# Sixteen key and value column tiles projected ahead of the attention, two at a time, with seven block products for eight

## The chip, the cores and the metric

The kernel runs on one core of one Trainium2 chip. The metric is the device time of one execution, in microseconds (us). Five engines work side by side, each through its own queue in order: TensorE (PE, matrix products into PSUM), VectorE (DVE), ScalarE (ACT), GpSimd (POOL), and SyncE (SP), which issues nearly all transfers between HBM and SBUF. An engine whose next instruction has to wait holds back everything that stands behind it in its queue.

## The reference

One encoder layer for 512 real and 16 meta tokens (528 rows, width 2048), all in float32:

```python
hn = rmsnorm(h, pre_norm_g[layer])
proj = jnp.einsum('bld,dc->blc', hn, w_in[layer])
qa, ka, va, ga, qb, kb, vb, gb = jnp.split(proj, SPLIT_POINTS, axis=-1)
ya = gqa_axial_mixer(qa, ka, va, ...) * jax.nn.silu(ga)
yb = diff_attn_mixer(qb, kb, vb, ...) * jax.nn.silu(gb)
y = jnp.einsum('blc,cd->bld', jnp.concatenate([ya, yb], axis=-1), w_out[layer])
h = h + rmsnorm(y, post_norm_g[layer])
return h[:, N_META:, :]
```

Mixer A has 8 query heads over 2 key heads, with a norm of each head's queries and keys and a rotary embedding. Mixer B has 8 heads of differential attention: two softmaxes per head, with a bias by distance, and the second is taken away from the first with a weight. Each head is 128 wide, so keys, values, queries and gates come as column tiles of 128: `T_KA`, `T_VA`, `T_GA`, `T_QB`, `T_KB`, `T_VB` and `T_GB` are the numbers of their first tiles in `w_t`.

## The kernel before

Every float32 product is made from two parts of each operand: a rounded one (`wh`, `xh`) and the rest (`wl`, `xl`). `three` (L174) issues the three products wh·xh, wh·xl and wl·xh. `xload` (L164) loads one of 16 blocks of the transposed input, 128x528, and splits it on ACT and DVE. `wload` (L142) loads a chunk of weights 128x1024 and splits it in the same way; three such chunks are held at a time, so the split of a chunk waits for PE to be done with the third one before it.

`dense_T` (L187) projects one column tile: two chunks, 16 blocks, and for keys and values (`KEYS`, all 528 tokens) two halves of 264 columns, 96 products in all; for queries and gates (`REAL`, 512 tokens) 48 products of 512 columns. After every group of three it calls `lanes.poll()`, which puts attention work on PE between them where a task is due. The tasks are Python generators (`attention_B` L420, `attention_A` L505, `p_times_v` L375, `finish_B` L468 and the turns of keys, values and queries). Each names by a number in `LAG` how much PE time is to pass before its next piece, by the planner's own clock, which sums planned PE times. `lanes.finish` forces a task: its pieces are then put one behind the other, with no projection between them.

The kernel has these stages:

- The start (L205-L215): the first key, query and gate tiles of head B0, while the 16 input blocks come in. Then the rows of `xn` are loaded (L238-L245, tile `xns`, four buffers), squared on ACT, and made into the row scales `rt` and, by a product with ones (`spread`, L258), into `rB`, with which every projected tile is multiplied. `spread` stands on PE between the two halves of the value tile of B0.
- Mixer B (L679-L689): for each head the gate tile, then value, key and query tiles of the next head, with the attention of the current head between their products.
- The keys and values of mixer A (L691-L695); then `queries_A` (L622) for a group of four heads, 192 products of 512 columns, with its norms and rotations on ACT, DVE and POOL.
- Mixer A (L697-L709): the heads run while the second group of queries and the eight gate tiles are projected, and into the first quarter of the output projection `dense_out` (L723).
- The rest of the output projection, the last norm and the residual.

A score step of mixer A (L527-L541) is: six products into the one pair of banks `sc`, a maximum on DVE, its scaling on POOL, the exponent on ACT, a reciprocal on DVE, and the scaling of `p` on POOL. Two steps make a half: their `p` are transposed on PE, split into `ph` and `pl` (ACT and DVE), and multiplied with the values (`pv`).

## Time and profile before

| what | value |
|---|---|
| time, median of 3 runs | 958.41 us (957.73 to 959.09) |
| the profiled execution's own time | 958.46 us |
| its span | 956.5 us, 13979 instructions |
| DVE busy | 525.5 us (55%), 900 instructions |
| ACT busy | 457.9 us (48%), 812 instructions |
| POOL busy | 127.7 us (13%), 211 instructions |
| chain that ended last | PE 89%, DVE 4%, ACT 2%, DMA 2%, POOL 2% |
| largest parts of that chain | PE pd L63 55%, PE po L63 19%, PE sc L63 6%, PE pv L63 5%, PE tr L66 5% |
| HBM read and written | 91.07 MB and 7.34 MB, 103 GB/s over the span |

The span is the time from the first to the last instruction of the one execution that the hardware profiler took. L63 and L66 are helpers in which all products and transposes are issued, so tiles tell them apart: `pd` is a projection, `po` the output projection, `sc` scores, `tr` transposes, `pv` p times values. Busy times of PE overlap a little, since products are pipelined; the pace of a long run of equal products is the better measure.

### The profile page before, as it was taken

The page shows a single profiled execution, that of the slowest core. Times are in us where ns is not written, and L with a number is a line of the kernel's source. Part 1 is how long each engine was busy: PE and PEld are TensorE (multiplying, and loading weights), DVE is VectorE, ACT ScalarE, POOL GpSimd, SP SyncE. Part 2 cuts the span into 40 slices and gives each one's busy share as a digit, 9 for nine tenths or more (in the row PEclk, how much of TensorE's full clock was granted, in tenths as well). Part 3 has the DMA queues.
Part 4 walks back from the last instruction along what each step waited for, and adds up shares of the span by engine and source line. Part 5 has one row for each costly group of instructions (what it writes and reads, how often), then busy time and mean ns, then how long its engine had stood idle before and what let it go on. Part 6 is the DMA issues. An engine that isn't in the chain of part 4 may idle for free.

```text
span 956.5 us, 13979 instructions
## 1 busy us (share of the span) xinstructions
PE 934.7 (98%) x5530; PEld 818.2 (86%) x5530; DVE 525.5 (55%) x900; ACT 457.9 (48%) x812; POOL 127.7 (13%) x211
## 2 busy tenths in 40 slices
PE   7999999999999999999999999998999999999996
PEld 6889898989989898998998888886888888888884
DVE  6276675747575574756654274447554663232325
ACT  6665555547464553746552253354555742221221
POOL 0001010101001010100201041225212120000002
PEclk9999999999999999999999999998999999999999
DMA  9752222322223122222223223111222344623314
GB/s 318 252 180 77 85 90 68 97 77 94 82 73 104 66 99 77 86 82 68 91 75 94 94 66 110 57 66 56 77 77 67 114 128 158 238 88 98 101 45 175
DMA packets 31426, 99.31 MB, mean 104 GB/s; under 512 B 3681, under 2 KB 5601, under 8 KB 30721
## 3 DMA queue, kind: packets, MB, share of 16 engines
q1 hardware_dynamic: 31216, 98.42, 31.1%
q8 instruction: 43, 0.70, 0.3%
q14 instruction: 23, 0.18, 0.1%
q10 hardware_dynamic: 144, 0.01, 0.0%
HBM read 91.07 MB, written 7.34 MB: 103 GB/s over the span
## 4 chain that ended last, share of the span: by engine, by line
PE 89%; DVE 4%; ACT 2%; DMA 2%; POOL 2%; issue 1%; SPq 0%; DVEq 0%; POOLq 0%; ACTq 0%
PE pd L63 55%; PE po L63 19%; PE sc L63 6%; PE pv L63 5%; PE tr L66 5%; DMA xns<-in_xn_dram 2%; DVE qn L567 1%; DVE wl L151 1%; POOL ssh L228 1%; ACT qn L639 0%; ACT jk L564 0%; PE ss L63 0%; POOL qn L581 0%; ACT p L537 0%; DMA gcol<-in_gpre_dram 0%
## 5 line engine op out<-in xcount | busy, mean ns | idle before, releaser
L63 PE MATMUL pd<-xh,wh 128*128 128x264 f32 (+1 forms) x992 | 334.8, 337 | 4.9 <-ACT wh L150 4.9
L63 PE MATMUL pd<-xh,wl 128*128 128x264 f32 (+1 forms) x992 | 326.4, 329 | 0.3 <-DVE wl L151 0.3
L63 PE MATMUL pd<-xl,wh 128*128 128x264 f32 (+1 forms) x992 | 326.1, 329 | 0.0
L150 ACT ACTIVATE wh<-st 128x1024 fp32r<-128x1024 f32 (+2 forms) x139 | 144.4, 1039 | 278.0 <-PE po L63 95.8
L151 DVE TENSOR_TENSOR wl<-st,wh 128x1024 fp32r<-128x1024 f32 (+2 forms) x139 | 167.2, 1203 | 176.0 <-ACT wh L150 174.7
L63 PEld LDWEIGHTS pd<-xh,wh 128*128 128x128 f32 x992 | 188.4, 190 | 17.6 <-ACT wh L150 4.9
L63 PEld LDWEIGHTS pd<-xh,wl 128*128 128x128 f32 x992 | 187.7, 189 | 18.0 <-DVE wl L151 0.7
L63 PEld LDWEIGHTS pd<-xl,wh 128*128 128x128 f32 x992 | 188.6, 190 | 11.6
L63 PE MATMUL po<-wh,ol 128*128 128x512 f32 x256 | 101.0, 395 | 0.9 <-DVE ol L296 0.9
L63 PE MATMUL po<-wl,oh 128*128 128x512 f32 x256 | 101.9, 398 | 0.0
L63 PE MATMUL po<-wh,oh 128*128 128x512 f32 x256 | 101.7, 397 | 0.0
L450 ACT ACTIVATE p<-p,mx 128x528 f32<-128x528 f32 x64 | 46.5, 728 | 34.2 <-POOL mx L447 34.0
L63 PEld LDWEIGHTS po<-wh,ol 128*128 128x128 f32 x256 | 48.1, 188 | 12.2 <-DVE ol L296 1.2
L440 DVE CUSTOM_DVE_ANT_0 p<-sc,dist 128x528 f32<-128x528 f32 x64 | 44.9, 701 | 24.0 <-PE sc L63 23.5
L63 PEld LDWEIGHTS po<-wl,oh 128*128 128x128 f32 x256 | 48.1, 188 | 11.2
L63 PEld LDWEIGHTS po<-wh,oh 128*128 128x128 f32 x256 | 48.1, 188 | 10.2
L63 PE MATMUL pd<-wh,xh 128*128 128x512 f32 x128 | 52.2, 408 | 0.8 <-DVE vf L287 0.8
L293 ACT ACTIVATE ph<-tr 128x512 fp32r<-128x512 f32 x64 | 37.6, 591 | 31.2 <-PE tr L66 30.9
L296 DVE TENSOR_TENSOR pl<-tr,ph 128x512 fp32r<-128x512 f32 x64 | 43.4, 688 | 16.1 <-ACT ph L293 14.9
L66 PE MATMUL tr<-ident,p 128*128 128x128 f32 (+1 forms) x320 | 50.8, 273 | 0.8 <-DVE pl L296 0.8
L63 PE MATMUL pd<-wh,xl 128*128 128x512 f32 x128 | 50.6, 395 | 0.0
L63 PE MATMUL pd<-wl,xh 128*128 128x512 f32 x128 | 50.5, 395 | 0.0
(161 smaller groups left out, 1292.1 us busy)
## 6 DMA issues: line engine op xcount, KB each, us to landing
st<-in_w_t_dram SPq DMA_DIRECT2D x82, 512.0 KB, 3.6
st<-in_w_o_dram SPq DMA_DIRECT2D x32, 512.0 KB, 3.6
st<-in_w_q_dram SPq DMA_DIRECT2D x16, 512.0 KB, 3.6
xs<-in_xT_dram SPq DMA_DIRECT2D x16, 264.0 KB, 5.1
xns<-in_xn_dram SPq DMA_DIRECT2D x8, 512.0 KB, 6.3
xr<-in_xn_dram SPq DMA_DIRECT2D x4, 1024.0 KB, 10.2
os<-oscr SPq DMA_DIRECT2D x6, 512.0 KB, 3.6
out_dram<-y SPq DMA_DIRECT2D x6, 512.0 KB, 2.7
```

Source lines behind the costliest of these rows:

```text
L63: self._add(self.nc.tensor.matmul(out, lhsT, rhs, start=start, stop=stop), us)
L66: self._add(self.nc.tensor.transpose(out, in_, ident), 0.109)
L150: nc.scalar.activation(wh[:, c], st[:, c], AF.Copy)
L151: nc.vector.tensor_tensor(out=wl[:, c], in0=st[:, c], in1=wh[:, c].bitcast(F32), op=ALU.subtract)
L228: nc.gpsimd.tensor_tensor(out=dst, in0=dst, in1=mhalf[:rows, :dst.shape[1]], op=ALU.pow)
L293: nc.scalar.activation(dst, src, AF.Copy)
L296: nc.vector.tensor_tensor(out=dst, in0=src, in1=h.bitcast(F32), op=ALU.subtract)
L440: nc.vector.tensor_tensor_reduce(out=two(p), in0=sc[:, :, :HALF], in1=two(dist[:, w0:w0 + NT]), scale=1.0, scalar=-3.0e38, op0=ALU.add, op ...
L450: nc.scalar.activation(p2[m], p2[m], AF.Exp, scale=0.125, bias=mx[:, m:m + 1], accum_out=sm[:, m:m + 1])
L567: nc.vector.scalar_tensor_tensor(out=raw[:, i, :], in0=raw[:, i, :], scalar=ss[:rows, i:i + 1], in1=g[:rows], op0=ALU.mult, op1=ALU.mult)
```

## The change

Two column tiles a and b are taken together as a matrix of weights with 2x2 blocks, and so is the input (even and odd blocks of 128 rows, first and second 264 tokens). Their projection is formed from seven products of blocks in place of eight, in Winograd's form of Strassen's method. This is done for eight pairs of tiles: keys and values of heads B1 to B7, and the two value tiles of mixer A. It is a stage of its own (`products`), ahead of all attention: its products have no `lanes.poll()` between them.

- In the start, `xsums` forms four sums of input blocks for each pair of blocks and splits them: POOL scales the raw blocks in place, DVE takes four differences of 264 columns, ACT rounds (`th`, 128x1056), and DVE takes the rest (`tl`). The raw block `xs` is now kept until then (five buffers in place of six); `xns` shares three buffers with these sums.
- `operands` loads quarter tiles (`rw`, every second piece of 128 columns, so pieces of 512 bytes), forms the sums of weights on POOL (two of 128x1024) and DVE (two), and splits seven operands for a pair. `product` runs 24 products of 264 columns.
- The seven results are added up on ACT and DVE, scaled by `rB` on POOL (two of 128x528 for a pair), and written to HBM (`pj`). The first key, query, value and gate tiles of B0 and gate A0 are written there too. The attention loads them from there (`got`, `gate_of`).
- The tables and the attention's buffers (`ap`, `psc`, `ptr`) are opened only after this stage, on the memory that it used.
- The eight gate tiles of mixer A move: A0 to the start, A1 to A6 into the heads of mixer B (`GATES_B`, spilled to HBM and loaded again), and A7 stays. `LATE` (an empty list) and `late_gate` go.

```diff
+GATE_0 = 0
+GATES_B = {0: 1, 1: 2, 2: 3, 3: 4, 4: 5, 5: 6}
 GATES = [[0, 1], [2, 3, 4, 5, 6, 7]]
...
+    def xsums(i, r1, r2):
+        with tc.high_priority(SUMS):
+            for k, r in ((2 * i, r1), (2 * i + 1, r2)):
+                nc.gpsimd.tensor_scalar(out=r, in0=r, scalar1=gcol[:, k:k + 1], scalar2=1.0,
+                                        op0=ALU.mult, op1=ALU.mult)
+            t = sp.tile([P, 4, HALF], F32, name="ts", tag="sb", bufs=3)
+            sub = lambda o, a, b: nc.vector.tensor_tensor(out=o, in0=a, in1=b, op=ALU.subtract)
+            sub(t[:, 0, :], r1[:, HALF:], r1[:, :HALF])
+            sub(t[:, 2, :], r2[:, HALF:], r1[:, HALF:])
+            sub(t[:, 1, :], r2[:, HALF:], t[:, 0, :])
+            sub(t[:, 3, :], t[:, 1, :], r2[:, :HALF])
+            nc.scalar.activation(th[i], t, AF.Copy)
+            nc.vector.tensor_tensor(out=tl[i], in0=t, in1=th[i].bitcast(F32), op=ALU.subtract)
...
-            st = ap.tile([P, 1024], F32, name="xns", tag="ph" if j else "pl")
+            st = sp.tile([P, 4 * HALF], F32, name="xns", tag="sb", bufs=3)[:, :1024]
...
+        a11 = raw(a, 0)
+        yield split(a11)
+        a21, a22 = raw(b, 0), raw(b, 1)
+        s1 = wp.tile([P, 1024], F32, name="s1w", tag="st")
+        nc.gpsimd.tensor_tensor(out=s1, in0=a21, in1=a22, op=ALU.add)
+        yield split(s1)
+        a12 = raw(a, 1)
+        s2 = wp.tile([P, 1024], F32, name="s2w", tag="st")
+        nc.vector.tensor_tensor(out=s2, in0=s1, in1=a11, op=ALU.subtract)
+        yield split(s2)
+        yield split(a12)
+        nc.gpsimd.tensor_tensor(out=a21, in0=a11, in1=a21, op=ALU.subtract)
+        yield split(a21)
+        yield split(a22)
+        nc.vector.tensor_tensor(out=a12, in0=a12, in1=s2, op=ALU.subtract)
+        yield split(a12)
...
+        for a, b in quads:
...
+            nc.scalar.activation(u1, product(b11), AF.Copy)
+            p5 = product(lambda i: sums(i, 0))
+            tt(out=u2, in0=product(lambda i: sums(i, 1)), in1=u1, op=ALU.add)
+            tt(out=ca[:, H0], in0=product(b21), in1=u1, op=ALU.add)
+            tt(out=u3, in0=product(lambda i: sums(i, 2)), in1=u2, op=ALU.add)
+            tt(out=cb[:, H1], in0=p5, in1=u3, op=ALU.add)
+            tt(out=ca[:, H1], in0=p5, in1=u2, op=ALU.add)
+            tt(out=cb[:, H0], in0=u3, in1=product(lambda i: sums(i, 3)), op=ALU.subtract)
+            nc.gpsimd.tensor_tensor(out=cb, in0=cb, in1=rB, op=ALU.mult)
+            put(b, cb)
+            tt(out=ca[:, H1], in0=product(b22), in1=ca[:, H1], op=ALU.add)
+            nc.gpsimd.tensor_tensor(out=ca, in0=ca, in1=rB, op=ALU.mult)
+            put(a, ca)
...
+    with tc.tile_pool(name="w1", bufs=5) as w1:
+        products([(T_KB + h, T_VB + h) for h in range(1, NH)] + [(T_VA, T_VA + 1)])
+    pre.close()
...
         if h + 1 < NH:
-            pss = dense_T(KEYS)
+            pss = dense_T(REAL)
             if h:
                 finish_head(h - 1)
-            v = values(pss)
-            ks = keys_B(dense_T(KEYS))
-            qs = queries_B(dense_T(REAL))
+            v = values(got(T_VB + h + 1, "vf"))
+            ks = keys_B(got(T_KB + h + 1, "kf"))
+            qs = queries_B(scaled(pss))
+        if h in GATES_B:
+            spill_gate(GATES_B[h], gate(dense_T(REAL), "gs"))
```

Where the instructions stand, engine by engine, shows what the diff alone does not. On DVE, in the middle of the start, the queue before held only the rests of the input blocks (`xl`) and of the weight chunks (`wl`):

```order
L168 SCALAR_TENSOR_TENSOR xl_111<-xs,gcol,xh_95 128x528
L168 SCALAR_TENSOR_TENSOR xl_112<-xs,gcol,xh_96 128x528
L151 TENSOR_TENSOR wl<-st,wh 128x768
L168 SCALAR_TENSOR_TENSOR xl_113<-xs,gcol,xh_97 128x528
L168 SCALAR_TENSOR_TENSOR xl_114<-xs,gcol,xh_98 128x528
L151 TENSOR_TENSOR wl<-st,wh 128x768
```

At the same place it now also holds the differences (`ts`) and the rests of the sums (`tl`):

```order
L177 SCALAR_TENSOR_TENSOR xl_117<-xs,gcol,xh_101 128x528
L191 TENSOR_TENSOR ts<-ts,xs 128x264
L191 TENSOR_TENSOR ts<-xs 128x264 x2
L177 SCALAR_TENSOR_TENSOR xl_118<-xs,gcol,xh_102 128x528
L191 TENSOR_TENSOR ts<-xs,ts 128x264
L197 TENSOR_TENSOR tl_135<-ts,th_127 128x1056
L160 TENSOR_TENSOR wl<-st,wh 128x768
```

Between two weight chunks stand five more instructions, and they stand ahead of the chunk; counted over the whole queue, 27 differences and 6 rests of sums stand ahead of the last chunk of the start.

On SP, at the end of the start, two chunks of `w_t` and then the rows `xns` stood behind the last chunk of `w_s`:

```order
L139 DMA st<-in_w_s_dram 128x768
L139 DMA xs<-in_xT_dram 128x528
L148 DMA st<-in_w_t_dram 128x1024 x2
L139 DMA xns<-in_xn_dram 128x1024 x8
L139 DMA xns<-in_xm_dram 16x1024 x2
```

Now three chunks stand ahead of the first row tile and a fourth behind it:

```order
L148 DMA st<-in_w_s_dram 128x768
L148 DMA xs<-in_xT_dram 128x528
L157 DMA st<-in_w_t_dram 128x1024 x3
L148 DMA xns<-in_xn_dram 128x1024
L157 DMA st<-in_w_t_dram 128x1024
L148 DMA xns<-in_xn_dram 128x1024 x7
L148 DMA xns<-in_xm_dram 16x1024 x2
```

There are three buffers `st`, so the third of these chunks needs the buffer of the last chunk of `w_s`, which is free when its `wl` is made.

On PE, in mixer A behind the second group of queries, groups of three projection products (`pd`) stood between scores, transposes and `pv` all through:

```order
L63 MATMUL sc<-kl,qh 128x264
L63 MATMUL sc<-kh,qlA 128x264
L63 MATMUL pd<-wh,xh_99 128x512
L63 MATMUL pd<-wh,xl_115 128x512
L63 MATMUL pd<-wl,xh_99 128x512
L63 MATMUL pv<-ph,vh 128x256
```

In the changed kernel the same stage reads:

```order
L68 MATMUL sc<-kl,qh 128x264
L68 MATMUL sc<-kh,qlA 128x264
L71 MATMUL tr<-ident,p 128x128 x8
L71 MATMUL tr<-ident,p 32x128 x2
L68 MATMUL sc<-kh,qh 128x264
L68 MATMUL sc<-kl,qh 128x264
L68 MATMUL sc<-kh,qlA 128x264
L68 MATMUL sc<-kh,qh 128x264
L68 MATMUL sc<-kl,qh 128x264
L68 MATMUL sc<-kh,qlA 128x264
L68 MATMUL pv<-ph,vh 128x256
```

From the end of the second group's products to the gate tile A7, 13 score steps, 91 products with values (seven groups of 13) and 74 transposes stand on PE with no `pd` among them.

## The prediction

> **What bounds the kernel now.** I read the page first, then PE's chain in order of time, then busy times by stage.

> ```profile
> span 956.5 us, 13979 instructions
> PE 934.7 (98%) x5530; PEld 818.2 (86%) x5530; DVE 525.5 (55%) x900; ACT 457.9 (48%) x812; POOL 127.7 (13%) x211
> 69.64 2.92 PE pd L63 x24
> 307.20:363.10 55.90, 55.90 (x375) 51.19 (x374) 35.69 (x65) 30.24 (x49) 6.03 (x11) 1.00 0.25 85
> 579.50:660.00 80.50, 76.46 (x407) 63.72 (x406) 39.60 (x73) 36.18 (x91) 24.04 (x41) 0.96 0.21 70
> ```

> PE is busy from end to end; 24 products of 264 columns take 2.92 us, 0.1217 each. The last two rows are stretches, with the busy times of PE, its weight loads, DVE, ACT and POOL in that order, then the granted clock. A head of mixer B (55.9 us) shows no idle PE; behind the second group of queries (579.5 to 660) PE misses 4.0 us. So a product less is time less, as long as PE has other products while the other engines do the softmax. Those are what this change takes out of the attention.

> **Products.** 16 tiles x 96 = 1536 products of 264 columns become 8 pairs x 7 x 24 = 1344; all others keep number and shape. 192 x 0.1217 = **-23.4 us**.

> **The start.**

> ```profile
> 30.07 0.96 DVE L151 TENSOR_TENSOR wl<-st,wh 128x768 fp32r<-128x768 f32 x1 [1.93 <-ACT wh L150]
> 4.46:31.03 26.57, 26.14 (x131) 22.66 (x132) 18.87 (x25) 16.47 (x24) 0.00 (x0) 1.00 0.87 316
> 51.13 0.77 DVE L287 TENSOR_TENSOR kf<-pd,rB 128x264 f32<-128x264 f32 x2
> L151 DVE TENSOR_TENSOR wl<-st,wh 128x1024 fp32r<-128x1024 f32 x130 | 159.4, 1226 | 168.7 <-ACT wh L150 167.5 <-PE tr L66 0.3
> 605.89 0.71 POOL L540 TENSOR_SCALAR p<-p,smA 128x528 f32<-128x528 f32 x1 [1.12 <-DVE smA L539]
> 27.19 11.36 SPq L139 DMA_DIRECT2D xns<-in_xn_dram  x8
> 50.77 0.39 PE L63 MATMUL sc<-xh,wh 128*128 128x264 f32 x1
> ```

> DVE ended the last rest of a `w_s` chunk at 31.03, having worked 18.9 us of the 26.6 before. Now 27 differences and 6 rests of sums stand ahead of it. Two operations of 264 columns took 0.77 us, so a difference is about 0.39; a rest of 1056 columns is 1.226 x 1056/1024 = 1.26. Together 10.5 + 7.6 = 18.1 us. If DVE keeps some 2 us of its idle time (its first transfers), it ends that rest at 4.5 + 18.9 + 18.1 + 2 = 43.5. POOL scales 16 blocks of 128x528 at 0.71 each, about 11 of them in between. Whether they stop DVE these shapes don't show; the nearest rows say yes:

> ```profile
> 599.57 1.22 DVE L151 TENSOR_TENSOR wl<-st,wh 128x1024 fp32r<-128x1024 f32 x1
> 599.81 1.03 POOL L534 TENSOR_SCALAR mxA<-mxA 128x1 f32<-128x1 f32 x1 [3.06 <-DVE mxA L533]
> 604.58 0.19 POOL L534 TENSOR_SCALAR mxA<-mxA 128x1 f32<-128x1 f32 x1 [1.91 <-DVE mxA L533]
> 558.14 1.14 DVE L567 SCALAR_TENSOR_TENSOR qn<-qn,ssh,gqB 128x128 f32<-128x128 f32 x4 [6.57 <-POOL ssh L228]
> 559.99 1.92 DVE L567 SCALAR_TENSOR_TENSOR qn<-qn,ssh,gqB 128x128 f32<-128x128 f32 x3
> 560.15 1.34 POOL L581 TENSOR_TENSOR qn<-qn,cosT 128x512 f32<-128x512 f32 x1 [0.52 <-DVE t L579]
> ```

> A POOL operation of one column, 0.19 us alone, took 1.03 and ended with DVE's `wl`; three DVE operations that take 0.29 each took 1.92 beside a POOL operation of 1.34. So I add 11 x 0.71 = 7.8: 51.3. [...]

> Behind that rest, on SP, stand a third `w_t` chunk and then the row tiles. Their first issue moves from 27.2 to about 51.5 (44 if POOL stops nobody). From it to PE's first product behind `spread` were 50.77 - 27.19 = 23.6 us. The chain is the same, with three buffers in place of four and one weight split that waits for PE among the squares; I keep its length. PE resumes at 75 in place of 50.8, and has nothing else there, since `spread` stands in its queue: **+24 us**, bounds 17 (POOL stops nobody) and 30 (three more rounds of transfer and square).

> **The block products.** A pair needs PE for 168 x 0.1217 = 20.4 us. On DVE stand nine operations of 128x1024 at 1.23 (11.1 us) and seven of 264 from PSUM (2.7); POOL has two of 1024 and two of 528, by the 1.34 for 512 columns 8.1 us. The first and the last exclude each other: 19.2 of 20.4 us. So PE stays the bound, if narrowly; **+3 us**, bounds 0 and 12 (if DVE's 2.7 come on top, 1.5 for each of eight pairs). The loads in pieces of 512 bytes are not in the trace; they have most of a pair's time to land, so I price them at nothing.

> **Into mixer B.** The attention's buffers wait until the last tile is written to HBM; then SP issues nine transfers before the values of B0 can come.

> ```profile
> oscr<-gA SPq DMA_DIRECT2D x4, 256.0 KB, 2.0
> 42.48 0.42 SPq L139 DMA_DIRECT2D cosT<-in_cos_dram  x1
> 61.45 0.44 PE tr L66 x4
> ```

> From PE's last block product: 0.4 (DVE) + 1.4 (POOL) + 2.4 (write) + 9 x 0.42 + 2.5 (landing) = 10.5 us. PE has 18 products of 512 columns (4.2 us) ahead of the transposes: **+6 us**, bounds 4 and 11 (the splits of queries and keys behind the loads).

> **Mixer A.** Seven of eight gate tiles are gone from here, so 13 score steps stand on PE without a projection between them.

> ```profile
> 602.93 0.39 PE L63 MATMUL sc<-kh,qlA 128*128 128x264 f32 x1 [0.22 <-DVE qlA L296]
> 603.40 0.28 PE L63 MATMUL sc<-kh,qlA 128*128 128x264 f32 x1
> 603.79 0.71 DVE L533 TENSOR_REDUCE mxA<-sc 128x1 f32<-128x528 f32 x1 [0.91 <-PE sc L63]
> 604.80 0.70 ACT L537 ACTIVATE p<-sc,mxA 128x528 f32<-128x528 f32 x1 [2.65 <-POOL mxA L534]
> L293 ACT ACTIVATE ph<-tr 128x512 fp32r<-128x512 f32 x64 | 37.6, 591 | 31.2 <-PE tr L66 30.9
> L296 DVE TENSOR_TENSOR pl<-tr,ph 128x512 fp32r<-128x512 f32 x64 | 43.4, 688 | 16.1 <-ACT ph L293 14.9
> 662.20 0.73 PE sc L63 x6
> 665.73 0.71 PE pv L63 x6
> 645.41 0.29 PE L63 MATMUL sc<-kh,qlA 128*128 128x264 f32 x1
> 652.50 0.80 ACT p L537 x2
> ```

> A step's products began at 602.93 and its banks were free at 605.50 (the exponent's end): 2.6 us to the next. Its `p` was scaled at 606.60 (605.89 + 0.71), 3.7 us after its start. For a half: 2.6 to the second step, + 0.6 because a `ph` of the half before stands ahead of the exponent on ACT; then 3.7, + 0.7 because a `pl` stands ahead of the maximum on DVE: 7.6 us. 13 steps are 6.5 halves, 49.4 us. PE's own work there is 13 x 0.73, 91 products of `pv` at 0.118 and 74 transposes at 0.11: 28.4. Beside the first steps run the norms and rotations of the second group; before, one step's exponent came 7.1 us after its last product (645.41 to 652.50) and not 1.4 (from the last product's start at 603.40 to 604.80). Two steps like that are 11; I take 9. 49.4 + 9 - 28.4 = 30.0, less the 4.0 that PE missed there before: **+26 us**. Bounds: 8, if only DVE's own work there counts (some 40 us: 13 maxima and 13 `pl` at 0.7, the norms, rotations and small rests); 30 without that rebate.

> **What else is forced.** The ends of B7 and A7 (`tr`, `pv` and `ss` in one piece) wait for `ph` and `pl` (1.3 us) some four times: **+6 us**, bounds 0 and 14.

> **The clock.**

> ```profile
> 653.34 1.69 PE sc L63 x6
> 655.03 1.28 PE pd L63 x3
> 666.44 0.70 PE pd L63 x3
> 656.74 5.47 PE pd L63 x18
> 648.00:660.00 12.00, 8.71 (x31) 6.86 (x32) 7.97 (x18) 3.90 (x12) 8.37 (x13) 0.72 0.13 44
> ```

> After PE waited 3 us at 650, six score products took 1.69 in place of 0.73, three projections 1.28 in place of 0.70, and 18 took 5.47 where six times 0.70 are 4.2: 2.8 us lost, at a mean clock of 0.72. I count two such waits, at `spread` and into mixer B: **+6 us**; bounds 0 and 15 (five, if mixer A repeats it). [...]

> **Sum.** -23.4 + 24 + 3 + 6 + 26 + 6 + 6 = +47.6 on the execution of 958.46 (its span and 2 us around it; the median, 958.41, is the same): **1006 us**. All low ends give -23.4 + 29 = +6, all high ends +89.

> **Rivals.**
> - POOL and DVE don't exclude each other here: the start costs 17, the block products nothing, mixer A some 5 less. 1006 - 7 - 3 - 5 = 991. For it: most POOL rows at 0.71 beside a busy DVE; against: the three pairs of rows above. [...] Chance 0.2.
> - DVE and POOL bound the block products (19.2 of 20.4 us leaves 6%), and the start takes its long chain: +9 and +6, 1021. For it: a wait of DVE for a POOL result holds the splits behind it. Chance 0.15.
> - Mixer A at DVE's floor, 8 in place of 26: 988. It needs scores that run ahead of the transposes, and PE's queue forbids it. Chance 0.06.
> - Faster: instructions in a queue overlap so far (four of L567 in 1.14) that DVE makes the sums in its idle 7.7 us and ahead of PE. It decides at the last `w_s` rest: made by 34, the row tiles come early enough and the start costs about 3; the same overlap puts mixer A at its floor of 8 and the rest at nothing but 3 into mixer B. -23.4 + 3 + 8 + 3 = -9: 949. Against: the sums alone are 18.1 us of rows that are nearly paces. Chance 0.06; with some part failing, no change, 0.03.

> **How the numbers follow.** The forecast has 0.5. The range takes in the first three rivals and most of the bounds: 970 to 1040. 0.2% (2 us) is about what a measurement of this kernel can tell from no change. Faster 0.06, same 0.03, slower 0.91.

> **What would show it.** Right: the first `xns` issue near 51, PE idle for over 10 us ahead of `spread`, projections resuming near 75; a pair in about 20.8 us; a wait of some 6 us at the first `tr` of B0; about 58 us in mixer A from the second group's last product to gate A7's first. Wrong: a last `w_s` rest before 38, or a stage without projections that takes under 40 us.

## The result

The changed kernel takes 1080.54 us (median of 4 runs, 1076.03 to 1081.13) beside 958.07 us for the kernel before: a ratio of 1.127, with a 95% interval of 1.124 to 1.130. It is 122 us slower. The forecast was 1006, with a range of 970 to 1040. The sign was right; the size was off by a factor of 2.6.

From the page of the changed kernel: span, busy times, granted clock in 40 slices, and the shares of the chain that ended last.

```profile
span 1078.6 us, 14007 instructions
PE 955.1 (89%) x5338; PEld 820.1 (76%) x5338; DVE 633.0 (59%) x1007; ACT 498.0 (46%) x853; POOL 222.2 (21%) x259
PEclk9869999999799899999989898999979999999999
PE 63%; DVE 15%; DMA 6%; ACT 5%; issue 5%; POOL 4%; SPq 0%; DVEq 0%; POOLq 0%; ACTq 0%
```

PE was on 89% of that chain before and is on 63% now. PE's busy time even rose by 20 us with 192 products fewer, since products at a lower granted clock last longer: the changed kernel's block products, of 264 columns, begin 0.121 us apart at a clock of 1.00 and 0.220 at 0.50 (medians), and the clock is 0.946 over this execution, 0.995 over that of the kernel before. So busy times cannot say where the time went. I made a ledger instead. For each PE instruction of the two traces I took its start, less the sum of the paces of all PE instructions ahead of it (0.1217 us for 264 columns, 0.233 for 512, 0.118 for 256, 0.11 for a transpose). What grows in it is time in which PE waited or ran slowly. The paces add up to 924.9 us before and 901.6 after. The losses, by stage:

| from, to | lost before | lost after | more | term of the prediction |
|---|---|---|---|---|
| start, to `spread` | 9.4 | 33.7 | 24.3 | 24 |
| to the first block product (before: to the values of B0) | 1.5 | 2.4 | 0.9 | part of the clock's 6 |
| block products | - | 21.5 | 21.5 | 3 |
| into mixer B, to the first transposes of values | - | 12.7 | 12.7 | 6 |
| heads of mixer B, to the `ss` of B6 | -0.2 | 37.8 | 38.0 | none |
| B7, keys and queries of mixer A | 2.6 | 14.9 | 12.3 | 6, with the last row |
| mixer A, to the first `po` | 6.9 | 32.5 | 25.6 | 26 |
| output projection | 2.6 | 12.6 | 10.0 | see above |

Less the 23.4 us of products saved, the differences come to 121.9 us; the spans differ by 122.1. Two rows were missed by far, the block products and the heads of mixer B; the way into mixer B and the ends (the last row and that of B7) came out at two to four times their terms.

**Block products.** The timeline around one pair's end; "[1.73 <-DVE wl]" is PE's idle time and what ended it.

```profile
222.94 2.39 POOL L351 TENSOR_TENSOR s1w<-rw 128x1024 f32<-128x1024 f32 x1 [8.31 <-DMA rw<-in_w_t_dram]
225.37 1.23 DVE L355 TENSOR_TENSOR s2w<-s1w,rw 128x1024 f32<-128x1024 f32 x1 [2.71 <-POOL s1w L351]
225.41 3.42 POOL L358 TENSOR_TENSOR rw<-rw 128x1024 f32<-128x1024 f32 x1
226.51 3.40 DVE L336 TENSOR_TENSOR wl<-rw,wh 128x1024 fp32r<-128x1024 f32 x1
229.97 0.39 PE L68 MATMUL pq<-xh,wl 128*128 128x264 f32 x1 [1.73 <-DVE wl L336]
```

Three operations that read two SBUF tiles each come one behind the other: DVE's `s2w` (1.23), POOL's difference, issued at 225.41 beside `s2w`, and DVE's `wl`. I read their lengths as the second beginning only when the first has ended, and the third only when the second has: 3.42 is then 1.2 of waiting and 2.2 of work (an estimate from these rows; POOL's sum of the same shape took 2.39 with DVE idle), and the `wl` takes 3.40, where the next one, at 230.98, takes 1.21. The prediction had taken this from rows of other shapes, and this trace agrees. This `wl` is the one that the pair's seventh product waits for. A wait of this kind stands in seven of the eight pairs (1.70 to 2.83 us, behind a `wl` of 3.38 to 3.41).

**Heads of mixer B.** DVE and PE in one head:

```profile
497.44 3.38 DVE L646 RECIPROCAL sq<-sq 128x128 f32<-128x128 f32 x4
503.52 0.76 DVE L619 SCALAR_TENSOR_TENSOR p<-p,c 128x528 f32<-128x528 f32 x1
504.19 2.78 DVE L443 TENSOR_TENSOR l<-qf,q 64x512 fp32r<-64x512 f32 x4
507.00 0.69 DVE L443 TENSOR_TENSOR pl<-tr,ph 128x512 fp32r<-128x512 f32 x1
507.75 0.61 PE L71 MATMUL tr<-ident,p 128*32 128x128 f32 x2 [4.07 <-DVE pl L443]
```

From 497.4 to 507.7 DVE has no pause: the reciprocals of the last head's norm, a `pl`, the query tile, the last `p`, four query rests, and only then the `pl` that frees the bank PE waits for. The same wait of 4.05 to 4.08 us stands at 457.27, 557.12 and 607.25. In the kernel before, the projections of values and keys (23 us of PE) stood ahead of the query tile in every head.

**Into mixer B.** SP's transfers, and PE's wait for the values of B0:

```profile
286.73 0.43 SPq L505 DMA_DIRECT2D gB<-pj  x1
287.21 0.90 SPq L584 DMA_DIRECT2D dist<-in_bias_dram  x2
292.88 3.21 SPq L432 DMA_DIRECT2D vf<-pj  x2
295.69 1.09 PE L71 MATMUL tr<-ident,vf 128*128 128x128 f32 x4 [12.52 <-DMA vf<-pj]
```

The values have the third tile of a tag with two buffers (`tT`; a tag is a set of buffers that tiles take in turn): their load is issued at 292.88, when the keys' splits are done, and not at 287.2.

**Mixer A.** A stretch of heads in mixer B, and the stretch of mixer A with no projections between the scores, as windows (busy PE, its weight loads, DVE, ACT, POOL; granted clock; DMA):

```profile
548.00:598.00 50.00, 45.95 (x230) 38.05 (x230) 32.41 (x60) 31.40 (x51) 5.56 (x10) 0.93 0.29 88
773.00:834.00 61.00, 37.85 (x249) 32.58 (x248) 39.31 (x84) 26.75 (x81) 26.63 (x44) 0.89 0.11 35
```

In mixer A it is 61 us from the second group's last product to the first of gate A7, where 58 were forecast: 32 us lost there, where the prediction had 30.

### The profile page after: what moved, and what is told of

It is laid out like the page before. It is cut to its first block, busy times and chain, and to the rows that moved or that the text cites. A ratio compares the mean times of both kernels' runs of the same rounds, so it can differ in the third digit from the quotient of the medians.

```text
span 1078.6 us, 14007 instructions
## 1 busy us (share of the span) xinstructions
PE 955.1 (89%) x5338; PEld 820.1 (76%) x5338; DVE 633.0 (59%) x1007; ACT 498.0 (46%) x853; POOL 222.2 (21%) x259
## 4 chain that ended last, share of the span: by engine, by line
PE 63%; DVE 15%; DMA 6%; ACT 5%; issue 5%; POOL 4%; SPq 0%; DVEq 0%; POOLq 0%; ACTq 0%
PE pd L68 28%; PE po L68 16%; PE pq L68 6%; PE sc L68 5%; PE pv L68 4%; PE tr L71 3%; DVE wl L336 3%; DMA rw<-in_w_t_dram 3%; PE p L68 2%; DVE sq L646 2%; DMA xns<-in_xn_dram 1%; DVE l L443 1%; DVE pl L443 1%; DVE ts L191 1%; DVE wl L160 1%
## 5 line engine op out<-in xcount | busy, mean ns | idle before, releaser
L68 PE MATMUL pd<-xh,wh 128*128 128x512 f32 (+1 forms) x464 | 185.4, 400 | 5.0 <-ACT wh L159 5.0
L68 PE MATMUL pd<-xh,wl 128*128 128x512 f32 (+1 forms) x464 | 178.1, 384 | 6.9 <-DVE wl L160 6.9
L68 PE MATMUL pd<-xl,wh 128*128 128x512 f32 (+1 forms) x464 | 178.5, 385 | 0.0
L68 PEld LDWEIGHTS pd<-xh,wl 128*128 128x128 f32 x464 | 91.3, 197 | 25.7 <-DVE wl L160 8.1
L68 PEld LDWEIGHTS pd<-xh,wh 128*128 128x128 f32 x464 | 91.8, 198 | 17.6 <-ACT wh L159 5.0
L68 PEld LDWEIGHTS pd<-xl,wh 128*128 128x128 f32 x464 | 92.1, 198 | 10.1
L336 DVE TENSOR_TENSOR wl<-rw,wh 128x1024 fp32r<-128x1024 f32 x40 | 66.1, 1653 | 17.0 <-ACT wh L335 17.0
L68 PE MATMUL pq<-tl,wh 128*128 128x264 f32 x256 | 72.8, 284 | 0.0
L68 PE MATMUL pq<-th,wh 128*128 128x264 f32 x256 | 72.7, 284 | 0.0
L68 PE MATMUL pq<-th,wl 128*128 128x264 f32 x256 | 72.6, 283 | 0.0
## 6 DMA issues: line engine op xcount, KB each, us to landing
xr<-in_xn_dram SPq DMA_DIRECT2D x4, 1024.0 KB, 10.7
```

Of the source, the lines that this page charges most:

```text
L68: self._add(self.nc.tensor.matmul(out, lhsT, rhs, start=start, stop=stop), us)
L336: nc.vector.tensor_tensor(out=wl, in0=t, in1=wh.bitcast(F32), op=ALU.subtract)
```

## The experiments

All are edits of the changed kernel, and line numbers are those of each run's own code. Unless an interval is given, a time is that of one execution, beside the kernel before (956.9 to 959.1 us). The block products' stage, where its code is the same, lost between 17.7 and 22.1 us from run to run, so differences of 4 us in the total mean little; the verdicts rest on the stages' ledger and on rows.

### POOL's difference goes to DVE

```diff
-        nc.gpsimd.tensor_tensor(out=a21, in0=a11, in1=a21, op=ALU.subtract)
+        nc.vector.tensor_tensor(out=a21, in0=a11, in1=a21, op=ALU.subtract)
```

> The one POOL difference of weights that runs beside a rest (a21 from a11, 3.42 us beside a wl of 3.40) goes to DVE, where it stands behind that wl. Theory 'port': POOL and DVE exclude each other, and the wl that the seventh product waits for takes 3.40 instead of 1.23 for that reason alone; then it takes 1.2, the wait of 1.7 to 2.8 us before the seventh product goes, a pair falls from about 22.5 us to 20.6 or so, and the time falls by 12 to 17 us. Rival 'order': the wl is late because DVE has the difference s2w ahead of it, which waits for a load and for POOL; then the wait shrinks by less than half and the time falls by under 7 us, or rises, since DVE has 1.2 us more to do in each pair.

1059.98 us, 20.5 less. The stage lost 2.8 us in place of 21.5; all other stages stayed within 2 us. The same place in its timeline:

```profile
214.67 1.23 DVE L355 TENSOR_TENSOR s2w<-s1w,rw 128x1024 f32<-128x1024 f32 x1 [3.27 <-POOL s1w L351]
215.81 1.22 DVE L336 TENSOR_TENSOR wl<-rw,wh 128x1024 fp32r<-128x1024 f32 x1
216.95 1.22 DVE L358 TENSOR_TENSOR rw<-rw 128x1024 f32<-128x1024 f32 x1
```

`s2w` still waits for POOL's sum, and still stands ahead of the `wl`; only the 3.40 has become 1.22, and the waits are gone. So it was POOL beside DVE (theory 'port') and not the order. Two other `wl` of each pair still take 2.0 and 2.3 us beside POOL's scalings of results, and cost PE next to nothing there. It beat the 12 to 17 us expected because the lower clock behind the waits went too: the stage's granted clock rose from 0.96 to 1.00.

### A sixth buffer for the quarter tiles

```diff
-    with tc.tile_pool(name="w1", bufs=5) as w1:
+    with tc.tile_pool(name="w1", bufs=6) as w1:
```

> Six buffers for the quarter tiles of weights in place of five. Theory 'port': loads are not the cause, the wl beside POOL's difference still takes 3.4 us; POOL's operations come earlier by some us and may fall beside another rest, so the time changes by less than 6 us either way. Rival 'order': the load of the next pair waits for a buffer, DVE's s2w waits for it, and the wl behind s2w is late by that; with a sixth buffer the load comes a product earlier, the wait of 1.7 us per pair goes, and the time falls by 12 to 17 us.

1091.65 us, 11 more: neither theory had that. The stage lost 34.3 us. Its timeline:

```profile
248.17 1.33 POOL L406 TENSOR_TENSOR C<-C,rB 128x528 f32<-128x528 f32 x1
248.25 2.33 DVE L355 TENSOR_TENSOR s2w<-s1w,rw 128x1024 f32<-128x1024 f32 x1 [2.90 <-POOL s1w L351]
249.46 3.33 POOL L358 TENSOR_TENSOR rw<-rw 128x1024 f32<-128x1024 f32 x1
250.50 3.37 DVE L336 TENSOR_TENSOR wl<-s2w,wh 128x1024 fp32r<-128x1024 f32 x1
```

The loads and POOL's sum come earlier, as meant. Now a scaling of a result falls beside `s2w` (2.33 in place of 1.23) and the difference beside `wl<-s2w`: two lengthened operations in one chain, and PE waits 2.94 us for this `wl` (2.2 to 3.1 in seven of the eight pairs). This speaks for theory 'port' as well: where POOL's work falls decides the price (a stage's loss of 34.3 us here, 21.5 in the changed kernel).

### `spread` behind gate A0

```diff
-    vB0 = dense_T(KEYS, p0(2), spread)
+    vB0 = dense_T(KEYS, p0(2))
+    gA0 = dense_T(REAL, p0(1))
+    spread(vB0[1])
```

> The product that spreads the row scales stands behind the second half of the value tile and behind gate tile A0 (96 products, 17 us), not between the halves; its second piece uses free columns of a projection's bank. Theory: PE's wait at the start is nothing but this place in its queue, while the row loads run; 17 of the 24 us go, less a little for a pause between the first products and the chunk behind them: the time falls by 13 to 18 us. Rival: the chunks' loads and splits for these 96 products stand behind the row tiles on SP or on ACT, so PE waits for them instead, and the time falls by under 6 us.

1070.07 us, 10.5 less, between the two. PE now works while the rows load: losses up to the first block product are 23.1 in place of 36.1 us. But the stage behind it lost 28.5 in place of 21.5, all of the difference in its first pair (10.7 in place of 3.2). The quarter tiles are loaded into the memory that the start used, so their first load is issued once the rows are done, and PE comes there sooner. It waits 4.85 us ahead of the stage's first product, and then 1.61 and 1.92 us for the second operand:

```profile
74.83 4.78 SPq L344 DMA_DIRECT2D rw<-in_w_t_dram  x4
80.68 0.59 PE L68 MATMUL pq<-xh,wh 128*128 128x264 f32 x1 [4.85 <-ACT wh L335]
```

### A third buffer for the tiles that come back

```diff
-        t = ap.tile([P, NT], F32, name=name, tag="tT")
+        t = ap.tile([P, NT], F32, name=name, tag="tT", bufs=3)
```

> Three buffers in place of two for the tiles that come back from HBM (tT). Theory: at the entry into mixer B the values of B0 are loaded only after the splits of keys have freed a buffer (issue at 292.9, the one before at 286.7), and PE waits for them 12.5 us; with a third buffer the load is issued at about 287, the wait falls by 4 to 6 us, and in the heads the loads also come earlier, which changes nothing there: the time falls by 4 to 7 us. Rival: the splits of queries and keys on ACT and DVE (both start at 290.7) hold the transposes' eviction and the scores anyway; the time falls by under 2 us.

1073.63 us, 6.9 less. The loss on the way into mixer B fell from 12.7 to 9.6 us: the mechanism expected, but 3.0 us where 4 to 6 were expected. The other 3.8 us are the scatter of the block products. The load of the values is now issued third of the tiles that come back, among nine other transfers, and PE's first transpose of them begins 6.2 us behind the issue. In the changed kernel, where the load came last, it was 2.8 (landing 2.67), and two loads of the same kind in the midst of that burst, `qf` and `gB`, took 5.0 and 5.2 us to land. From the run with three buffers:

```profile
281.78 0.43 SPq L432 DMA_DIRECT2D vf<-pj  x1
288.00 1.08 PE L71 MATMUL tr<-ident,vf 128*128 128x128 f32 x4 [9.50 <-DMA dist<-in_bias_dram]
```

### Only heads B1 to B3 and the values of mixer A ahead

```diff
-        products([(T_KB + h, T_VB + h) for h in range(1, NH)] + [(T_VA, T_VA + 1)])
+        products([(T_KB + h, T_VB + h) for h in range(1, 4)] + [(T_VA, T_VA + 1)])
...
+            v = values(here(pss, "vf") if late else got(T_VB + h + 1, "vf"))
+            ks = keys_B(here(dense_T(KEYS), "kf") if late else got(T_KB + h + 1, "kf"))
+            qs = queries_B(scaled(dense_T(REAL) if late else pss))
```

> Only B1 to B3 and the values of mixer A are made by seven products ahead; keys and values of B4 to B7 are projected inside mixer B as in the kernel before, the gates of mixer A stay where the change put them. Theory 'filler': in a head whose next keys and values are projected beside it PE has 24 us more of products and loses nothing, so the losses of heads 4 to 6 (5.4 to 8.8 us each by PE's ledger, some 25 us with the end of mixer B) go; four pairs fewer lose 4 x 2.7 us less in the block products and cost 4 x 2.92 us more products: in all 20 to 30 us less than the changed kernel's 1080. Rival 'own pace': the loss per head comes from the order on DVE whatever PE does beside it; then only the block products change and the time stays within 8 us of 1080.

1050.88 us, 29.7 less. From the `ss` of B2 to that of B6 the loss was 1.0 us in place of 27.7. A window over these heads:

```profile
392.00:593.90 201.90, 200.98 (x1266) 180.45 (x1265) 116.25 (x203) 102.49 (x159) 13.23 (x30) 1.00 0.27 89
```

PE is busy for 201 of 202 us. A head whose next keys and values are projected beside it hides its softmax wholly; the same four heads lost 5.6 to 8.8 us each in the changed kernel.

### The gates of mixer A stay in mixer A

```diff
-GATES_B = {0: 1, 1: 2, 2: 3, 3: 4, 4: 5, 5: 6}
+GATES_B = {}
```

> Gate tiles A1 to A6 stay in mixer A, as before; only A0 goes ahead. Theory 'filler': mixer A has its six gate tiles (67 us of products) back and loses under 8 us there instead of 33, but heads 0 to 5 of mixer B have 11.2 us less each, their softmax does not get shorter, and each loses 6 to 11 us more: +36 to +66 in B, -25 in A, in all 10 to 40 us slower than 1080. Rival 'pile': a head of mixer B loses a fixed 5 to 7 us at one place (the reciprocals and the query rests on DVE ahead of a pl that PE waits for), whatever stands beside it; then B keeps its loss and the time falls by 20 to 30 us.

1062.90 us, 17.6 less. Mixer A lost 10.1 us in place of 32.5: the missing gate tiles were 22 of the 26 us that it lost more than before. The output projection lost 6.0 in place of 12.6, so half of that row comes from them too. The heads of mixer B lost 46.3 in place of 37.8 us: 11.7 in the first (5.8 in the changed kernel) and 5.5 to 6.3 in each of the others, with 11 us of products fewer beside each. In time that is near the rival's result (20 to 30 us less), and the filler theory, by which B would lose 36 to 66 us more, is too simple. The rival's picture isn't confirmed either: the waits of 4.07 us for `pl` are gone there, and behind the first head several of 1.4 us and less for other results of DVE stand in their place. What a head loses depends on the order that comes about, not on the amount of products alone.

### Without the reciprocals of mixer B

```diff
-        for t in range(TT):
-            tq = slice(t * P, (t + 1) * P)
-            nc.vector.reciprocal(out=sq[:, tq], in_=sq[:, tq])
```

> The four reciprocals of the last norm of a head of mixer B (3.38 us on DVE for a head) are left out, so that head's norm multiplies by the root instead. Theory 'pile': they stand at the head's end ahead of the pl that PE waits for (4.07 us idle at 507.75); without them that wait falls under 1.5 us and the time falls by 15 to 27 us over eight heads. Rival: the query rests and the other pieces there hold the pl anyway, or DVE's whole load sets the head's length: the time falls by under 8 us.

1056.42 us, 24.1 less. The heads of mixer B lost 20.4 in place of 37.8 us, and the wait that was 4.07 is now:

```profile
498.16 0.39 PE L71 MATMUL tr<-ident,p 128*32 128x128 f32 x2 [1.46 <-DVE pl L443]
```

The pile theory's number (under 1.5 us) holds at all four places where the wait was over 4 us. In one head a wait of 2.73 us for a `pl` (at 405.99) came where the changed kernel has none.

### Gate tiles ahead of the queries

```diff
+        if h in GATES_B:
+            spill_gate(GATES_B[h], gate(dense_T(REAL), "gs"))
         if h + 1 < NH:
             pss = dense_T(REAL)
...
-        if h in GATES_B:
-            spill_gate(GATES_B[h], gate(dense_T(REAL), "gs"))
```

> In heads 0 to 5 of mixer B the gate tile of mixer A is projected ahead of the query tile of the next head in place of behind it; nothing else moves. Theory 'place': a head loses 5 to 7 us because the query rests, the turn of the values and the last norm of the head before come upon DVE together (22 us into the head); with the queries 11 us later the norm is done before they come, heads 1 to 5 lose under 3 us each, head 6 and the end of mixer B lose the same as before: the time falls by 12 to 22 us. Rival: the sum of DVE's work in a head is what holds PE, and the loss turns up at another place: within 5 us of 1080.

1060.82 us, 19.7 less. No work was removed, only its order changed. The heads of mixer B lost 25.8 in place of 37.8 us; head 6, which has no such gate, still lost 10.6. Some heads kept more than the 3 us expected (4.2 and 4.3). Of the rest, 3.7 us came in the block products and is scatter.

### Eight ordinary products ahead

```diff
-        xsums(k0 // 2, r1, r2)
...
-    with tc.tile_pool(name="w1", bufs=5) as w1:
-        products([(T_KB + h, T_VB + h) for h in range(1, NH)] + [(T_VA, T_VA + 1)])
+    for ct in ahead:
+        put_plain(ct, dense_T(KEYS, p0(2)))
```

> The sixteen tiles are projected ahead by the ordinary eight products (96 of 264 columns each, whole chunks), with no sums of inputs or weights. It has 192 products more than the changed kernel (23.4 us). Theory: the start loses some 22 us less, the block products' stage 21 us less (no POOL beside DVE), the rest as in the changed kernel (about 100 us over before): 1055 to 1065. So the seven products cost about 20 us more than they save. Rival: the stage loses as much with ordinary products, because loads and evictions set its pace, and the time is above 1080.

1058.71 us. This splits the change into its two ideas. Projecting sixteen tiles ahead, with the gate tiles moved as the change moves them, costs about 100 us over the kernel before, with no product saved. Seven products for eight save 23.4 us of paces and still make it 21.8 us slower again: 21.7 in the start (loss to `spread` 12.0 without sums, 33.7 with them) and 21.5 in the stage, which here shows no idle PE. With POOL's difference moved to DVE the seven products came to 1059.98, so then the two forms cost about the same. Of this run, the start and the stage:

```profile
0.00:51.90 51.90, 42.83 (x241) 37.73 (x241) 25.15 (x41) 33.81 (x51) 1.59 (x7) 0.99 0.83 291
75.00:255.00 180.00, 180.00 (x1492) 180.00 (x1491) 50.03 (x62) 32.89 (x31) 0.00 (x0) 1.00 0.33 115
```

### Without POOL's scaling in the start

```diff
-            for k, r in ((2 * i, r1), (2 * i + 1, r2)):
-                nc.gpsimd.tensor_scalar(out=r, in0=r, scalar1=gcol[:, k:k + 1], scalar2=1.0,
-                                        op0=ALU.mult, op1=ALU.mult)
```

> The scaling of the 16 raw blocks on POOL is left out, so the sums are of unscaled blocks. Theory 'port': in the start POOL's scalings and DVE's differences exclude each other; without them DVE ends the last rest of the start's weights some 5 to 8 us earlier, the spread product comes at 66 to 69 instead of 73.6, and the time falls by 5 to 8 us. Rival: the differences and rests alone (18 us on DVE) and three buffers for rows and sums set it; then spread comes at 72 or later and the time falls by under 2.5 us.

1073.95 us, 6.6 less. The first row load and `spread`, here and in the changed kernel (its first load was issued at 48.19):

```profile
40.39 0.42 SPq L148 DMA_DIRECT2D xns<-in_xn_dram  x1
65.49 2.61 PE L68 MATMUL tr<-dg,ones 128*128 128x512 f32 x4 [15.42 <-DVE rm L273]
```

```profile
73.60 2.07 PE L68 MATMUL tr<-dg,ones 128*128 128x512 f32 x2 [15.71 <-DVE rm L276]
```

8.1 us earlier, at the upper edge of what theory 'port' expected. In the seven other runs whose start has the changed kernel's code `spread` came at 71.9 to 73.3, so the gain is 6.4 to 8.1. Leaving the scaling out also takes away a result that the differences wait for, a rival cause. The rows decide: in the changed kernel DVE has no pause from 27 to 55 us, and its operations are longer beside POOL's, up to the last rest of `w_s`:

```profile
43.05 1.20 DVE L191 TENSOR_TENSOR ts<-xs 128x264 f32<-128x264 f32 x2
45.08 1.85 POOL L188 TENSOR_SCALAR xs<-xs,gcol 128x528 f32<-128x528 f32 x1 [1.12 <-DVE xl L177]
46.36 1.37 DVE L160 TENSOR_TENSOR wl<-st,wh 128x768 fp32r<-128x768 f32 x1
```

Without the scaling the same two took 0.77 and 0.95, and the last rest ended 7.8 us earlier (39.94 and 47.73):

```profile
37.95 0.77 DVE L188 TENSOR_TENSOR ts<-xs 128x264 f32<-128x264 f32 x2
38.99 0.95 DVE L160 TENSOR_TENSOR wl<-st,wh 128x768 fp32r<-128x768 f32 x1
```

### Four edits together

POOL's difference on DVE, `spread` later, three buffers, and gates ahead of the queries.

> Four of the edits in one kernel: POOL's difference on DVE, spread behind gate A0, three buffers for the tiles that come back, gate tiles of mixer A ahead of the queries. If their causes are apart, their gains add: 20 + 10 + 5 + 12 to 22, so 1023 to 1033; still above the kernel before, since mixer A keeps its 33 us without products beside it, and the start and the two turns of stages some 35. If they share a wait, it stays above 1040.

1039.65 us (median of 4 runs, 1038.03 to 1042.23), a ratio of 1.086 to the kernel before, interval 1.084 to 1.088. That is 41 us less than the changed kernel, but 7 to 17 us short of the 47 to 57 that the sum had. By the ledger the four took 47 us from their stages when they stood alone. Six of these are lost in the block products: with `spread` later they lost 9.1 us and not 2.8, because the first quarter tiles are late there whoever makes the difference. It is still 81 us behind the kernel before; no version found beats that.

## Why the prediction was wrong

**Right.** The products saved (23.4 against 23.4 us). The start: 24.3 against 24. POOL's share of it was put at 7.8 us, and without the scaling the last rest of `w_s` ended 7.8 us earlier. But that 24 was met so closely is partly luck: the rest ended at 47.7, not 51.3, since DVE's own part was 3.6 us shorter than estimated, and from the first row load to `spread` it took 25.4 us, not the 22.1 of before, so two errors cancel. Mixer A: 25.6 against 26 us, 61 us of stretch against 58, and with the gates put back the loss is nearly that of before (10.1 and 6.9). Here too two small differences meet: 32 us lost in the stretch and not 30, and 6.9 and not 4.0 before. Working each score step out as a chain of rows, and not as a share of DVE's time, gave the second. The rival that POOL and DVE do not exclude each other fell three times over: a `wl` of 3.40 us became 1.22 when POOL's operation beside it went (`sub_on_dve`), an `s2w` of 1.23 became 2.33 when one came beside it (`six_loads`), and a rest of 1.37 became 0.95 without the scaling (`no_scaling`).

**Heads of mixer B: no term in the sum.** This is the largest error and the main step that failed: the sum puts the heads at nothing, and they lost 38 us. The first part of the prediction said that a product less is time less "as long as PE has other products while the other engines do the softmax". I then checked that condition for mixer A, where the projections vanish altogether, and not for mixer B, where they shrink from 45.7 us a head (192 products of 264 columns, 96 of 512) to 33.6 (144 of 512). The busy shares look harmless: DVE has 32.4 of 50 us. But the losses come from bursts. With the keys and values gone, the query tile follows close upon the norm of the head before, and 10 us of DVE work stand ahead of one `pl`. Three runs show the parts: keys and values beside the head take the loss away, leaving the reciprocals out takes 17 us of it, and another order of the same work takes 12. How the rest splits among DVE's other pieces stays open.

**The block products: +3, measured +21.5.** The mechanism was named, and its price was taken as an average: 19.2 us of DVE and POOL in 20.4 of PE. The step that failed is "so PE stays the bound, if narrowly", and its bound of 12. What decided here is which DVE operation stands directly behind POOL's. It is the rest that PE needs next, and it loses 2.2 us in seven of the eight pairs (3.38 to 3.41 for 1.22); then the granted clock falls behind some of the waits (0.61 over the 4 us behind one of 1.73). Moving one POOL operation ends it.

**Into mixer B: 6, measured 12.7.** I counted nine transfers and missed that the values are the third tile of a tag with two buffers, so that their load waits for the keys' splits. A third buffer brought 3.0 us of it back. Of the rest, the landing was put at 2.5 us, and with a third buffer, among the other transfers, it was 6.2 us from the issue to PE's first transpose.

**The ends: 6, measured 22.3** for B7 and for A7 with the output projection. No run takes them apart as a whole. The first runs into the same forced pieces as the heads; `queries_last`, which does not touch it, left it as it was. Of the second, half went when six gate tiles were put back (`gates_stay`).

**The clock.** It was a term of its own (6 us for two waits). There were many more waits than two: behind the first 20 us the trace of the changed kernel has 119 us at half clock, that of the kernel before 13. The cost lies within the stages' losses above.

## What to carry to other kernels

Work taken away from the bottleneck engine saves time only where that engine still has other work at each burst of the others: with keys and values beside them, the four heads up to the `ss` of B6 lost 1.0 us here, and 27.7 without. So lay the new order of every stage beside the bursts, burst by burst, and do not compare mean shares. Where two engines hold each other up, as POOL and DVE do here (a `wl` of 3.40 us for 1.22), ask which operation comes second and who waits for it; an average over the stage says little. A rearranged sum of fewer products must also pay for its operands: here the sums of inputs and weights cost 43 us to save 23, and still 24.5 when one of them had moved to another engine.

## What the runs showed of the hardware

Equal waits of PE do not cost the same. Windows of 4 us behind two waits of the block products in the changed kernel, of 1.80 and 1.73 us:

```profile
162.70:166.70 4.00, 4.00 (x33) 4.00 (x34) 3.97 (x8) 1.06 (x1) 1.45 (x1) 1.00 0.54 144
230.10:234.10 4.00, 4.00 (x22) 4.00 (x23) 3.53 (x6) 0.00 (x0) 1.49 (x1) 0.61 0.52 140
```

33 products are counted in the first window and 22 in the second: the granted clock stayed at 1.00 or fell to 0.61. Of the six waits of 1.70 to 1.88 us three were followed by the lower clock and three were not, and from one pair's wait to the next it was 24.05 to 25.04 us with the lower clock in between and 22.34 to 22.52 without.

```profile
227.55:230.97 3.42, 1.69 (x14) 1.48 (x13) 3.39 (x4) 1.06 (x1) 1.28 (x1) 1.00 0.00 0
230.97:234.38 3.41, 3.41 (x18) 3.41 (x17) 2.70 (x4) 0.17 (x1) 1.77 (x1) 0.50 0.66 177
```

```profile
174.38:177.79 3.41, 1.71 (x15) 1.49 (x13) 3.41 (x2) 1.06 (x1) 3.31 (x2) 1.00 0.21 79
177.79:181.21 3.42, 2.39 (x19) 2.39 (x20) 3.39 (x4) 0.00 (x0) 0.00 (x0) 1.00 0.00 0
181.21:184.62 3.41, 3.41 (x30) 3.41 (x29) 2.66 (x3) 1.06 (x1) 0.00 (x0) 1.00 0.22 65
```

The wait of 1.80 us at 162.60 lies within one step too, and the clock stayed at 1.00: between 1.5 and 2.0 us these records, in which the ends of products are modelled, do not tell the two cases apart. The scatter of 17.7 to 22.1 us in the block products may come from where the waits fall among the steps; no run shows that.

POOL's sum of two 128x1024 tiles took 2.39 us with DVE idle, and its difference of the same shape shows 3.42 us. It was issued 1.2 us before `s2w` ended, so the rest is about 2.2, an estimate from these two rows: this long POOL row is one that seems to wait within its own time.
